# A two-layer decoder trunk on one core: the FFN's hidden tile turned by DMA in 16 bit halves in place of TensorE, tiles on multiples of 512 bytes, and a new rule for the pinned order

## The chip, the cores and the metric

The kernel runs on one core of a Trainium2 chip. A core has a matrix engine (TensorE, PE in the profile, with its weight loads as PEld), a vector engine (DVE), an activation engine (ACT), a general engine (POOL, nearly unused here) and a queue engine (SP) that issues most transfers. The metric is the device time of one execution in microseconds; smaller is better. A program of one core shows times that agree closely from run to run.

## The reference

The input x is 256 tokens by 2048 features, float32. There are two layers. Each adds a token mixer and then a dense SwiGLU FFN to the residual, with an RMS norm ahead of each; a last norm ends the trunk. Layer 0 mixes by causal pooling over windows of 2, 4, 8 and 16 tokens, layer 1 by differential attention with ALiBi.

```python
for i in range(DEPTH):
    hn = rmsnorm(h, norm_mix[i])
    mix = pool_mixer(...) if i % 2 == 0 else diff_attention(...)
    h = h + mix
    h = h + swiglu(rmsnorm(h, norm_ffn[i]), w_gate[i], w_up[i], w_down[i])
return rmsnorm(h, final_norm)

def swiglu(h, wg, wu, wd):          # wg, wu: 2048 x 5632, wd: 5632 x 2048
    return (jax.nn.silu(h @ wg) * (h @ wu)) @ wd
```

The FFNs hold most of the work: 176 of the 328 weight steps belong to gate and up, 88 to down.

## The kernel before

**Products.** Each weight matrix is read once, in steps of 1 MiB (`raw`, 128 partitions x 4 blocks x 512 columns): two slices of 128 rows of the weights, each with a left and a right 512 columns. Every operand is split into a high part, rounded for the fast float32 mode of TensorE, and a low part (what is left), and a product of two blocks is three matmuls: high by high, high by low, low by high (line 380). ACT rounds the high part (line 313), DVE subtracts it (line 314). A plain step is eight block products, 24 matmuls of 128x512. A step "by seven" follows Strassen's scheme: seven block products, 21 matmuls, for sums of weights that DVE makes (lines 319 to 321) and ACT and DVE split (lines 327, 328), and for sums of the activations made ahead. Which steps go by seven is fixed by lists, `GATE_UP`, `SEVEN_DOWN` and others, so that PE's time and DVE's are near each other.

**Groups.** `group` runs over the six or eight steps of one pair of 512 output columns and leaves eight PSUM banks; `combined` (lines 400 to 411: two copies on ACT, eight operations on DVE) makes four 128x512 blocks of them, `c11` to `c22`, for two halves of the tokens. The next group writes the same banks.

**FFN.** `ffn` goes over 11 groups of gate and up in chunks of 4, 4 and 3. After each group it computes silu(gate) on ACT (line 677) and the product with up on DVE (line 678), in token order, in place. The down product needs h with features on the partitions, so `pair` turns it: eight transposes of 128x128 on TensorE against the identity into a PSUM bank (line 450), then either ACT's cast and DVE's subtraction into the tile `h` (lines 454, 455), or, for a tile that will go by seven, two copies into `e` (line 463), three DVE operations for the sums (464 to 466), and the split (467, 468). A group makes two h tiles. After each chunk two groups of the down product run over the chunk's h tiles and are added to the residual `x_tok` (line 700). The same `pair` turns the residual ahead of the FFNs and attention, and attention's output.

**Buffers and queues.** Three `raw` buffers, three pairs of split weights, one set of sums. All weight loads are issued by SP (line 307). A load waits until DVE has read the buffer that it fills.

**Order.** The program's order is not that of the text. `in_order_of_need` reads the finished list of instructions, `steps_of` finds what depends on what, `walk` plays the list forward with fixed costs for each instruction, picking on each engine the ready instruction of lowest rank, and `due` works out by when each is needed, from PE's sequence. ACT, DVE and POOL are ranked by that due time, PE and SP by the order of the text. Two rounds are made, the shortest walk is kept, and its sequence is pinned on PE, DVE, ACT and SP. Each engine then runs its sequence strictly in turn, whatever becomes ready first on the chip.

**Places in memory.** Pools lie one behind the other. Those of the start (`st`) and of attention (`ap_`) begin with, or hold, small tiles: `counts` of 32 bytes a partition, `small` of 256.

Of the kernel before, what the change touches and what calls it, by code (L numbers as in the profile page):

```python
# [10 lines left out]
F32 = mybir.dt.float32  # L11
F32R = mybir.dt.float32r
AF = mybir.ActivationFunctionType
ALU = mybir.AluOpType
# [14 lines left out]
LATER = 70  # L29
ROUNDS = 2  # L30

# [22 lines left out]

A22, A21, A11, A12, S1, S3, S2, S4 = range(8)
T1, T3, T2, T4 = range(4)


# [5 lines left out]
LANDING = 2100  # L64
PER_MIB = 2500


class Step:

    def __init__(self, k, ins=None):  # L70
        self.k, self.ins, self.engine = k, ins, ins.engine if ins else POOL
        self.dma = bool(ins) and ins.opcode == "DMACopy"
# [6 lines left out]
        if self.dma:  # L79
            bytes_ = 4 * math.prod(c for _, c in ins.outs[0].ap)  # L80
            self.share = PER_MIB * bytes_ / 2 ** 20
            self.holds, self.lasts = (60 if self.engine == ACT else 330), LANDING + self.share
        elif self.engine == PE:
            n = size(ins.outs[0])
            one = 110 if ins.is_transpose else 14 + n / 2.4 if "float32r" in str(ins.ins[0].dtype) else 14 + n / 0.6
            self.holds, self.lasts = one, one + 163
        elif self.engine == DVE:
            if ins.opcode == "TensorScalarPtr":
                self.lasts = 185 + n / 0.96 if n > 8 else 159
            else:  # L90
                self.lasts = 152 + n / (1.92 if ins.opcode == "TensorCopy" else 0.96)
            self.holds = max(self.lasts - 80, 60)
        elif self.engine == ACT:
            self.lasts = 165 + n * 0.852
            if ins.opcode == "Activation" and any(hasattr(a, "ap") for a in list(ins.ins)[1:]):
                self.lasts += 100
            self.holds = max(self.lasts - 30, 60)
            if len(ins.outs) > 1:
                self.lasts, self.holds = self.lasts + 190, self.lasts + 160
        else:  # L100
            self.holds = self.lasts = 400


def steps_of(instructions):
# [3 lines left out]
    for ins in instructions:  # L108
# [15 lines left out]
        for writes, args in ((False, ins.ins), (True, ins.outs)):  # L124
            for a in args:
# [3 lines left out]
                t, dims = ap.tensor, [tuple(d) for d in ap.ap]  # L129
                first = ap.offset % dims[0][0]  # L130
                last = first + sum((c - 1) * s for s, c in dims[1:])
                alone = writes
                if t.space == PSUM:
                    first, last, alone = 0, 511, True
                if t.name not in seen:
# [76 lines left out]

def due(steps, start):

    by_start = sorted(steps, key=lambda s: start[s.k])
    at, clock = {}, 0.0
    for s in by_start:
        if s.engine == PE:
            at[s.k], clock = clock, clock + s.holds
    limit = [0.0] * len(steps)  # L220
    for s in reversed(by_start):
        limit[s.k] = min([limit[k] - s.lasts - SIGNAL[steps[k].engine] for k in s.after] + [at.get(s.k, clock)])
    return limit


def in_order_of_need(tc):

    steps = steps_of(list(tc.nc.cur_bb.bb.instructions))
    rank = [float(s.k) for s in steps]
    start, end = walk(steps, rank)  # L230
    for _ in range(ROUNDS):
# [14 lines left out]
def trunk_kernel(ctx, tc, x_n, gains, scale_in, final_in, subln, lam_in, band, counts_in, dist,  # L246
# [33 lines left out]
    ones = const.tile([P, P], F32, name="ones")  # L280
    nc.vector.memset(ones, 1.0)
    make_identity(nc, ident)
# [144 lines left out]

    def square_sum(ss, t, j):
# [16 lines left out]
    def pair(dst, src, gains, seven):  # L445

        ps = aux((P, 2, 2, P))
        for i in range(2):
            for t in range(2):
                nc.tensor.transpose(ps[:, i, 1 - t if seven else t], src(i, t), ident)  # L450
        if not seven:
# [9 lines left out]

        for i, at in ((0, slice(A21, A11 + 1)), (1, slice(A22, A12 + 1, A12 - A22))):
            nc.scalar.activation(e[:, at], ps[:, i], AF.Copy, scale=1.0 if gains is None else gains[i])
        nc.vector.tensor_tensor(e[:, S1:S3 + 1], e[:, A21:A11 + 1], e[:, A22:A21 + 1], ALU.subtract)
        nc.vector.tensor_tensor(e[:, S2], e[:, S1], e[:, A11], ALU.subtract)
        nc.vector.tensor_tensor(e[:, S4], e[:, A12], e[:, S2], ALU.add)
        nc.scalar.copy(dst[:, 0], e)  # L467
        nc.vector.tensor_tensor(dst[:, 1], e, f32(dst[:, 0]), ALU.subtract)

    def transposed(xp, j, gain, seven=()):  # L470
# [8 lines left out]
    with tc.tile_pool(name="start", bufs=1, reuse_waits="tile") as st:  # L479

        warm = tmp.tile([P, 8], F32, name="warm", bufs=1)
        nc.scalar.activation(warm[:, 0:1], ones[:, 0:1], AF.Sqrt)
# [35 lines left out]
        def squares(j):  # L518
            for t in range(2):
                square_sum(ss_in, t, j)  # L520

# [56 lines left out]
        def residual(g):  # L578

            cols = slice(g * 512, (g + 1) * 512)  # L580
            for t in range(2):
                z = st.tile([P, 512], F32, name="z", bufs=2)
                nc.vector.scalar_tensor_tensor(z, zp[g][t], counts[:, g, t:t + 1], scale_sb[:, cols], ALU.mult, ALU.mult)
                nc.vector.tensor_tensor(x_at(t, g * 512), z, x_at(t, g * 512), ALU.add)
                square_sum(ss, t, g)

# [41 lines left out]
    turn["of"] = 4  # L628
    nc.sync.dma_start(out=dist_sb, in_=dist)

    def finish(cs, ys, final_sb, ss):

        for t in range(2):
            part = tmp.tile([P, 64], F32, name="part", bufs=2)
            nc.vector.tensor_reduce(part[:, 0:1], ss[:, t, 0:2], AX.X, ALU.add)
            for b in range(2):
                for h in range(2):
                    first = 1024 + b * 512 + h * S
                    mine = slice(h * S, (h + 1) * S)
                    nc.vector.tensor_tensor(x_at(t, first, S), cs[t][b][:, mine], x_at(t, first, S), ALU.add)  # L640
                    sq = tmp.tile([P, 512], F32, name="sq", bufs=1)
# [15 lines left out]
    def ffn(layer, xq, ss, next_op, next_gain):  # L657
# [3 lines left out]
        with tc.tile_pool(name=f"ffn{layer}", bufs=1, reuse_waits="tile") as hp:  # L661
            g0 = 0
            ys = []
            for c, n in enumerate(CHUNKS):
# [6 lines left out]
                for g in range(g0, g0 + n):  # L671
# [3 lines left out]
                    for t in range(2):  # L675
                        gate, up = cs[t]
                        nc.scalar.activation(gate, gate, AF.Silu, scale=r[:, t:t + 1])  # L677
                        nc.vector.scalar_tensor_tensor(up, up, r[:, t:t + 1], gate, ALU.mult, ALU.mult)
                    for i in range(2):
                        at = 2 * (g - g0) + i  # L680
                        ht = hp.tile(pair_shape(at in SEVEN_DOWN), F32R, name="h", tag=f"h{at}")
                        pair(ht, lambda k, t: cs[t][1][:, (2 * i + k) * P:(2 * i + k + 1) * P], None, at in SEVEN_DOWN)
                        hp_tiles.append(ht)
                for o in range(2):
# [13 lines left out]
                    for b, t in ((0, 0), (0, 1), (1, 0), (1, 1)):  # L698
                        j = 2 * o + b
                        nc.vector.tensor_tensor(x_at(t, j * 512), cs[t][b], x_at(t, j * 512), ALU.add)  # L700
                        if last:
                            square_sum(ss_next, t, j)
                        if last and next_op is None:
# [15 lines left out]
    with tc.tile_pool(name="attn", bufs=1, reuse_waits="tile") as ap_, ExitStack() as heads:  # L719
        hq = heads.enter_context(tc.tile_pool(name="qk_sums", bufs=1, reuse_waits="tile"))  # L720
        at = heads.enter_context(tc.tile_pool(name="attn_tmp", bufs=2, reuse_waits="tile"))
        small = ap_.tile([P, 64], F32, name="small")
        qs_col, subln_sb, lam_sb, lp, le, neg_lam, gs = (
# [83 lines left out]
        for g in range(2):  # L807
            order, by_seven = LATE if g else EARLY
            cs = scaled(combined(group([(xp[p], p in by_seven, w_v[g, p]) for p in order], op_, bufs=1), op_), (r_col, r_col))
            for h in range(4 * g, 4 * g + 4):  # L810
# [6 lines left out]
                for t in range(2):  # L817
                    sq = tmp.tile([P, 512], F32, name="sq", bufs=1)[:, :E]
                    nc.scalar.activation(sq, op[:, t, :], AF.Square, accum_out=oss[:, t:t + 1])
# [7 lines left out]
        for g in range(2):  # L827
            cs = combined(group([(oT[p], p in SEVEN_O, w_o[g, p]) for p in range(NP)], op_, bufs=1), op_)
            for b in range(2):
                j = 2 * g + b  # L830
                for t in range(2):
                    nc.vector.tensor_tensor(x_at(t, j * 512), cs[t][b], x_at(t, j * 512), ALU.add)
                    square_sum(ss_next, t, j)
                transposed(xq, j, 4, SEVEN)
# [91 lines left out]
```

## Time and profile before

| | us |
|---|---|
| median of 3 runs | 1822.0 (1821.96 to 1822.05) |
| the profiled execution | 1821.8 |
| its span, first to last instruction | 1819.9 |
| start and pooling, to the first weight step of FFN 0 | about 39 |
| FFN 0 | about 39 to 738 |
| attention with its output product | about 738 to 1114 |
| FFN 1 and the end | about 1114 to 1820 |

In groups of instructions the columns are: line, engine, operation, tiles written and read, shape, count, then busy time and mean ns of one, then the engine's idle time ahead of them and what ended it. Matmuls overlap, so their mean is longer than the distance from one start to the next; the distance is read from the chain, where a run of matmuls stands as one piece with its length and count. In stretches, each engine has its busy time and, in brackets, the instructions that began in it. In waits the three numbers are the total in us, how many waits, and the longest. "SPq" is SP's queue of transfers; the row of an issue ends with KB of one transfer and the median us from issue to landing. TensorE's granted clock was 0.998 of full speed over the span.

### The profile page before, as it was taken

Reading aid. Unit: us, or ns where it says so; the run is one execution under the profiler, and the core shown is the slowest. Engines: PE = TensorE matmul, PEld = TensorE weight load, DVE = VectorE, ACT = ScalarE, POOL = GpSimd, SP = SyncE. Lnnn points to the kernel's source line nnn. Section 1 sums busy time; section 2 is a strip of 40 time slices with the busy share of each in tenths; the row PEclk is TensorE's granted clock in tenths of the full one; section 3 lists DMA queues with packets and bytes.
Section 4 is the critical chain, followed back from the end, with each engine's and each line's share of the span. In section 5 each row is a group of like instructions: output and inputs, shape, how many; then the busy total and the mean of one; then the engine's idle time right before and its main releaser. Section 6 shows DMA issues by size and latency. Waiting matters only on the chain.

```text
span 1819.9 us, 21122 instructions
## 1 busy us (share of the span) xinstructions
PE 1806.3 (99%) x8153; PEld 1487.6 (82%) x8153; DVE 1686.3 (93%) x1875; ACT 1084.0 (60%) x1170; POOL 0.7 (0%) x6
## 2 busy tenths in 40 slices
PE   9999999999999999999999999999999999999997
PEld 7888888888888888888888888888888888888886
DVE  7999999999999999989997889999999999999996
ACT  7656654565645566666666766665655556445663
POOL 0000000000000000000000000000000000000000
PEclk9999999999999999999999999999999999999999
DMA  6555555455555455635544445555555455555562
GB/s 267 208 185 207 187 208 208 185 208 215 201 209 187 182 208 185 225 145 185 185 176 172 184 165 194 196 208 185 214 207 203 185 208 192 210 222 192 196 220 109
DMA packets 50932, 356.37 MB, mean 196 GB/s; under 512 B 6160, under 2 KB 6288, under 8 KB 8464
## 3 DMA queue, kind: packets, MB, share of 16 engines
q1 hardware_dynamic: 49968, 353.40, 52.7%
q10 hardware_dynamic: 864, 1.63, 0.2%
q8 instruction: 64, 1.05, 0.2%
q14 instruction: 36, 0.29, 0.1%
HBM read 352.90 MB, written 2.10 MB: 195 GB/s over the span
## 4 chain that ended last, share of the span: by engine, by line
PE 98%; DVE 1%; ACT 1%; issue 0%; DVEq 0%; ACTq 0%
PE b L380 92%; PE b L450 2%; PE b L559 1%; PE b L555 1%; PE b L767 1%; PE b L798 0%; DVE wlo L314 0%; PE b L813 0%; PE b L485 0%; PE b L814 0%; PE b L530 0%; PE b L815 0%; DVE c L402 0%; DVE c L403 0%; PE b L752 0%
## 5 line engine op out<-in xcount | busy, mean ns | idle before, releaser
L380 PE MATMUL b<-whi,xp 128*128 128x512 f32 x2654 | 850.3, 392 | 0.4 <-ACT xp L467 0.3
L313 ACT CAST whi<-raw 128x1536 fp32r<-128x1536 f32 (+1 forms) x328 | 573.0, 1747 | 349.3 <-PE b L380 270.4
L314 DVE TENSOR_TENSOR wlo<-raw,whi 128x1536 fp32r<-128x1536 f32 (+1 forms) x328 | 681.3, 2077 | 69.6 <-ACT whi L313 68.4
L380 PEld LDWEIGHTS b<-whi,xp 128*128 128x128 f32 x2654 | 496.4, 188 | 104.9 <-DVE c L408 2.7
L380 PE MATMUL b<-wlo,xp 128*128 128x512 f32 x1327 | 520.1, 392 | 0.1
L327 ACT CAST thi<-tsum 128x1024 fp32r<-128x1024 f32 x254 | 266.3, 1052 | 183.9 <-DVE tsum L321 96.1
L380 PE MATMUL b<-whi,h 128*128 128x512 f32 x1108 | 349.2, 390 | 0.0
L328 DVE TENSOR_TENSOR tlo<-tsum,thi 128x1024 fp32r<-128x1024 f32 x254 | 306.5, 1216 | 2.3 <-ACT thi L327 2.0
L380 PEld LDWEIGHTS b<-wlo,xp 128*128 128x128 f32 x1327 | 249.2, 188 | 50.9 <-DVE wlo L314 0.5
L380 PE MATMUL b<-thi,xp 128*128 128x512 f32 x744 | 248.4, 390 | 0.0
L380 PEld LDWEIGHTS b<-whi,h 128*128 128x128 f32 x1108 | 207.6, 188 | 42.6 <-DVE c L408 0.2
L380 PE MATMUL b<-wlo,h 128*128 128x512 f32 x554 | 216.0, 390 | 0.1
L380 PEld LDWEIGHTS b<-thi,xp 128*128 128x128 f32 x744 | 139.4, 188 | 28.8 <-ACT thi L327 0.2
L319 DVE TENSOR_TENSOR tsum<-raw 128x1024 f32<-128x1024 f32 x127 | 154.5, 1216 | 0.6
L380 PE MATMUL b<-tlo,xp 128*128 128x512 f32 x372 | 144.9, 389 | 0.0
L380 PEld LDWEIGHTS b<-wlo,h 128*128 128x128 f32 x554 | 104.0, 188 | 21.9 <-DVE wlo L314 0.5
L320 DVE TENSOR_TENSOR tsum<-tsum,raw 128x512 f32<-128x512 f32 x127 | 86.7, 683 | 0.6
L321 DVE TENSOR_TENSOR tsum<-tsum,raw 128x512 f32<-128x512 f32 x127 | 86.7, 682 | 0.5
L380 PEld LDWEIGHTS b<-tlo,xp 128*128 128x128 f32 x372 | 69.8, 188 | 15.1
L380 PE MATMUL b<-thi,h 128*128 128x512 f32 x240 | 78.7, 389 | 0.0
L677 ACT ACTIVATE c<-c,r_tok 128x512 f32<-128x512 f32 x44 | 31.9, 724 | 63.1 <-DVE c L403 36.1
L380 PE MATMUL b<-whi,oT 128*128 128x512 f32 x216 | 69.0, 395 | 0.0
(148 smaller groups left out, 1230.7 us busy)
## 6 DMA issues: line engine op xcount, KB each, us to landing
raw<-w_gu SPq DMA_DIRECT2D x176, 1024.0 KB, 4.8
raw<-w_down SPq DMA_DIRECT2D x88, 1024.0 KB, 4.8
raw<-w_qk SPq DMA_DIRECT2D x32, 1024.0 KB, 4.8
raw<-w_v SPq DMA_DIRECT2D x16, 1024.0 KB, 4.8
raw<-w_o SPq DMA_DIRECT2D x16, 1024.0 KB, 4.7
x_tok<-x_n SPq DMA_DIRECT2D x4, 512.0 KB, 7.2
w<-pool_w SPq DMA_DIRECT2D x4, 512.0 KB, 7.7
raw<-pool_w SPq DMA_DIRECT2D x2, 1024.0 KB, 11.2
```

Source lines behind the costliest of these rows:

```text
L313: nc.scalar.copy(hi[:, lo_block:], raw[:, lo_block:])
L314: nc.vector.tensor_tensor(lo[:, lo_block:], raw[:, lo_block:], f32(hi[:, lo_block:]), ALU.subtract)
L319: nc.vector.tensor_tensor(s, raw[:, B11:B22 + 1], raw[:, B12:B12 + 1].broadcast_to([P, 2, 512]), ALU.add)
L320: nc.vector.tensor_tensor(t[:, 0], s[:, 0], raw[:, B22], ALU.add)
L321: nc.vector.tensor_tensor(t[:, 1], t[:, 0], raw[:, B21], ALU.add)
L327: nc.scalar.copy(hi, t)
L328: nc.vector.tensor_tensor(lo, t, f32(hi), ALU.subtract)
L380: nc.tensor.matmul(ps[b], x, y[:, block], start=first, stop=(left[b] == 0))
L450: nc.tensor.transpose(ps[:, i, 1 - t if seven else t], src(i, t), ident)
L555: nc.tensor.matmul(yp[g][t], a[:, rows], w_pool[g][:, at], start=(at == 0), stop=(at == 3))
L559: nc.tensor.matmul(yp[g][t], u, v[:, at], start=(at == 0 and j == 0), stop=(at == 3 and j == 2))
L677: nc.scalar.activation(gate, gate, AF.Silu, scale=r[:, t:t + 1])
```

## The change

1. In both FFNs h is no longer turned on TensorE. After the product with up, ACT copies the 128x512 block of floats, read as 16 bit halves, into the place of gate, low halves first and then high halves (`flip`). One DMA transpose, issued by SP, turns these 128 x 1024 halves into `turned`; a group has two, one for each half of the tokens. `pair_of_words` puts the halves together again by two ACT copies into `e` and goes on as before from there: cast and subtraction, or sums and split. All h tiles go through `e` now. The transposes of the residual and of attention's output stay on TensorE.
2. The eight slots of a tile that goes by seven have a new order.
3. `dist_sb` and `ones` move out of the constants, the tile `sq` out of `tmp`; squares are written to a tile of the start's pool, or over the block `c` just added to the residual; in the last group that is PSUM. `counts` and `small` are padded to 512 bytes a partition.
4. The order: `latest` plays the list backward from the end, engine by engine, in place of `due`. Eight rounds; in each, two ranks are tried, one with PE and SP by the order of the text, one with every engine by need, and the shorter walk goes on. Overlaps are found in bytes, the DMA transpose gets a cost, and ACT's reads with more than three dimensions get 80 ns more.

```diff
-ROUNDS = 2
+ROUNDS = 8
...
-A22, A21, A11, A12, S1, S3, S2, S4 = range(8)
+A12, A11, A21, A22, S3, S1, S2, S4 = range(8)
...
+PLACES = (slice(A11, A21 + 1), slice(A12, A22 + 1, A22 - A12))
...
+        if turns:
+            self.share = TURN_TILE * n * P / 2048
+            self.holds, self.lasts = 1290, 1000 + self.share
...
-def due(steps, start):
+def latest(steps, start):
+    missing = [len(s.after) for s in steps]
+    ready, place = [0.0] * len(steps), [0.0] * len(steps)
...
+        s = steps[-heapq.heappop(able[e])[1]]
+        place[s.k] = free[e] = now + s.holds
+        for k in s.before:
+            b = steps[k]
...
+            ready[k] = max(ready[k], place[s.k] + after)
...
+    end = max(place)
+    return [end - p for p in place]
...
     for _ in range(ROUNDS):
-        limit = due(steps, start)
-        rank = [float(s.k) if s.engine in (PE, SP) else limit[s.k] for s in steps]
-        again, span = walk(steps, rank)
+        need = latest(steps, last)
+        both = [[float(s.k) if s.engine in (PE, SP) else need[s.k] for s in steps], need]
+        last, span = min((walk(steps, r) for r in both), key=lambda w: w[1])
         if span < end:
-            start, end = again, span
+            start, end = last, span
...
-    dist_sb = const.tile([P, 2 * P], F32, name="dist_sb")
...
-        sq = tmp.tile([P, 512], F32, name="sq", bufs=1)
...
+    def half_words(ap):
+        return ap.bitcast(U16)
+
+    def flip(turned, t, gate, up):
+
+        halves_ = half_words(gate)
+        nc.scalar.copy(halves_.rearrange("p (w n) -> p w n", w=2), half_words(up).rearrange("p (n w) -> p w n", w=2))
+        nc.sync.dma_start_transpose(out=turned[:, t].rearrange("p w b n -> p (w b) n"), in_=halves_)
+
+    def pair_of_words(dst, turned, i, seven):
+
+        e = tmp.tile([P, 8, P], F32, name="e", bufs=1)
+        words = half_words(e).rearrange("p b (n w) -> p b n w", w=2)
+        if seven:
+            for k, at in enumerate(PLACES):
+                nc.scalar.copy(words[:, at], turned[:, :, :, 2 * i + k].rearrange("p t w n -> p t n w"))
+            seven_of(dst, e)
+            return
+        for k in range(2):
+            nc.scalar.copy(words[:, 2 * k:2 * k + 2], turned[:, :, :, 2 * i + k].rearrange("p t w n -> p t n w"))
+        both = e[:, :4].rearrange("p (k t) n -> p k (t n)", k=2)
+        nc.scalar.copy(dst[:, :, 0], both)
+        nc.vector.tensor_tensor(dst[:, :, 1], both, f32(dst[:, :, 0]), ALU.subtract)
...
-        counts = st.tile([P, 8], F32, name="counts")
+        counts = st.tile([P, 128], F32, name="counts")[:, :8]
...
-                    nc.scalar.activation(sq[:, :S], x_at(t, first, S), AF.Square, accum_out=part[:, at:at + 1])
+                    nc.scalar.activation(cs[t][b][:, mine], x_at(t, first, S), AF.Square, accum_out=part[:, at:at + 1])
...
                         nc.vector.scalar_tensor_tensor(up, up, r[:, t:t + 1], gate, ALU.mult, ALU.mult)
+                        if t == 0:
+                            turned = hp.tile([P, 2, 2, 4, P], U16, name="turned")
+                        flip(turned, t, gate, up)
...
-                        pair(ht, lambda k, t: cs[t][1][:, (2 * i + k) * P:(2 * i + k + 1) * P], None, at in SEVEN_DOWN)
+                        pair_of_words(ht, turned, i, at in SEVEN_DOWN)
...
-        small = ap_.tile([P, 64], F32, name="small")
+        small = ap_.tile([P, 128], F32, name="small")
+        dist_sb = ap_.tile([P, 2 * P], F32, name="dist_sb")
+        nc.sync.dma_start(out=dist_sb, in_=dist)
+        ones = all_ones(ap_)
```

More of the change, by code (lines that the diff above doesn't have):

```diff
@@ L12 @@
 F32R = mybir.dt.float32r
+U16 = mybir.dt.uint16
 AF = mybir.ActivationFunctionType
@@ L65 @@
 PER_MIB = 2500
+TURN_TILE = 14
 class Step:
@@ L71, in __init__ @@
         self.k, self.ins, self.engine = k, ins, ins.engine if ins else POOL
-        self.dma = bool(ins) and ins.opcode == "DMACopy"
+        turns = bool(ins) and ins.opcode == "DmaTransposeAnt"
+        self.dma = turns or bool(ins) and ins.opcode == "DMACopy"
         self.before, self.after, self.reads = set(), [], set()
@@ L78, in __init__ @@
         n = max(size(a) for a in list(ins.outs) + list(ins.ins) if hasattr(a, "ap"))
-        if self.dma:
+        if turns:
+            self.share = TURN_TILE * n * P / 2048
+            self.holds, self.lasts = 1290, 1000 + self.share
+        elif self.dma:
             bytes_ = 4 * math.prod(c for _, c in ins.outs[0].ap)
@@ L97, in __init__ @@
             self.holds = max(self.lasts - 30, 60)
+            if len(list(ins.ins[0].ap)) > 3:
+                self.lasts += 80
             if len(ins.outs) > 1:
@@ L129, in steps_of @@
                 t, dims = ap.tensor, [tuple(d) for d in ap.ap]
-                first = ap.offset % dims[0][0]
-                last = first + sum((c - 1) * s for s, c in dims[1:])
+                each = mybir.dt.size(a.dtype)
+                first = ap.offset % dims[0][0] * each
+                last = first + sum((c - 1) * s for s, c in dims[1:]) * each + each - 1
                 alone = writes
                 if t.space == PSUM:
-                    first, last, alone = 0, 511, True
+                    first, last, alone = 0, 2047, True
                 if t.name not in seen:
@@ L210, in walk @@
     return start, max(free.values())
-def due(steps, start):
[L215 to L223, printed above, removed]
+def latest(steps, start):
+    missing = [len(s.after) for s in steps]
+    ready, place = [0.0] * len(steps), [0.0] * len(steps)
+    engines = (PE, DVE, ACT, SP, POOL)
+    free = {e: 0.0 for e in engines}
+    able, coming = {e: [] for e in engines}, {e: [] for e in engines}
+    for s in steps:
+        if not s.after:
+            heapq.heappush(coming[s.engine], (0.0, s.k))
+    for _ in steps:
+        now, e = min((free[e] if able[e] else max(free[e], coming[e][0][0]), i)
+                     for i, e in enumerate(engines) if able[e] or coming[e])
+        e = engines[e]
+        while coming[e] and coming[e][0][0] <= now:
+            k = heapq.heappop(coming[e])[1]
+            heapq.heappush(able[e], (-start[k], -k))
+        s = steps[-heapq.heappop(able[e])[1]]
+        place[s.k] = free[e] = now + s.holds
+        for k in s.before:
+            b = steps[k]
+            if b.engine != e or b.dma:
+                after = b.lasts + SIGNAL[e] - (0 if b.dma else b.holds)
+            elif e == DVE or e == ACT and k in s.reads:
+                after = b.lasts + SETTLES[e] - b.holds
+            else:
+                after = 0.0
+            ready[k] = max(ready[k], place[s.k] + after)
+            missing[k] -= 1
+            if not missing[k]:
+                heapq.heappush(coming[b.engine], (ready[k], k))
+    end = max(place)
+    return [end - p for p in place]
 def in_order_of_need(tc):
@@ L230, in in_order_of_need @@
     start, end = walk(steps, rank)
+    last = start
     for _ in range(ROUNDS):
-        limit = due(steps, start)
-        rank = [float(s.k) if s.engine in (PE, SP) else limit[s.k] for s in steps]
-        again, span = walk(steps, rank)
+        need = latest(steps, last)
+        both = [[float(s.k) if s.engine in (PE, SP) else need[s.k] for s in steps], need]
+        last, span = min((walk(steps, r) for r in both), key=lambda w: w[1])
         if span < end:
-            start, end = again, span
+            start, end = last, span
     order = mybir.DependencyInfo(mybir.DependencyClass.NoSync, mybir.DependencyReason.DATA)
@@ L277, in trunk_kernel, with all_ones @@
     gain_sb = const.tile([P, 6, NK], F32, name="gain_sb")
-    dist_sb = const.tile([P, 2 * P], F32, name="dist_sb")
     ident = const.tile([P, P], F32, name="ident")
-    ones = const.tile([P, P], F32, name="ones")
-    nc.vector.memset(ones, 1.0)
+    def all_ones(pool):
+        ones = pool.tile([P, P], F32, name="ones")
+        nc.vector.memset(ones, 1.0)
+        return ones
     make_identity(nc, ident)
@@ L426, in rsqrt, with square_sum @@
         return r
-    def square_sum(ss, t, j):
-        sq = tmp.tile([P, 512], F32, name="sq", bufs=1)
+    def square_sum(ss, t, j, sq):
         nc.scalar.activation(sq, x_at(t, j * 512), AF.Square, accum_out=ss[:, t, j:j + 1])
@@ L449, in pair @@
             for t in range(2):
-                nc.tensor.transpose(ps[:, i, 1 - t if seven else t], src(i, t), ident)
+                nc.tensor.transpose(ps[:, i, t], src(i, t), ident)
         if not seven:
@@ L460, in pair, with seven_of @@
         e = tmp.tile([P, 8, P], F32, name="e", bufs=1)
-        for i, at in ((0, slice(A21, A11 + 1)), (1, slice(A22, A12 + 1, A12 - A22))):
+        for i, at in enumerate(PLACES):
             nc.scalar.activation(e[:, at], ps[:, i], AF.Copy, scale=1.0 if gains is None else gains[i])
-        nc.vector.tensor_tensor(e[:, S1:S3 + 1], e[:, A21:A11 + 1], e[:, A22:A21 + 1], ALU.subtract)
+        seven_of(dst, e)
+    def seven_of(dst, e):
+        nc.vector.tensor_tensor(e[:, S3:S1 + 1], e[:, A11:A21 + 1], e[:, A21:A22 + 1], ALU.subtract)
         nc.vector.tensor_tensor(e[:, S2], e[:, S1], e[:, A11], ALU.subtract)
@@ L479, in trunk_kernel @@
     with tc.tile_pool(name="start", bufs=1, reuse_waits="tile") as st:
+        ones = all_ones(st)
         warm = tmp.tile([P, 8], F32, name="warm", bufs=1)
@@ L519, in squares @@
             for t in range(2):
-                square_sum(ss_in, t, j)
+                square_sum(ss_in, t, j, st.tile([P, 512], F32, name="sq"))
         def turned(g):
@@ L584, in residual @@
                 nc.vector.tensor_tensor(x_at(t, g * 512), z, x_at(t, g * 512), ALU.add)
-                square_sum(ss, t, g)
+                square_sum(ss, t, g, st.tile([P, 512], F32, name="sq"))
         def onward(g):
@@ L628, in trunk_kernel @@
     turn["of"] = 4
-    nc.sync.dma_start(out=dist_sb, in_=dist)
     def finish(cs, ys, final_sb, ss):
@@ L701, in ffn @@
                         if last:
-                            square_sum(ss_next, t, j)
+                            square_sum(ss_next, t, j, cs[t][b])
                         if last and next_op is None:
@@ L817, in trunk_kernel @@
                 for t in range(2):
-                    sq = tmp.tile([P, 512], F32, name="sq", bufs=1)[:, :E]
+                    sq = at.tile([P, E], F32, name="sq", bufs=1)
                     nc.scalar.activation(sq, op[:, t, :], AF.Square, accum_out=oss[:, t:t + 1])
@@ L832, in trunk_kernel @@
                     nc.vector.tensor_tensor(x_at(t, j * 512), cs[t][b], x_at(t, j * 512), ALU.add)
-                    square_sum(ss_next, t, j)
+                    square_sum(ss_next, t, j, cs[t][b])
                 transposed(xq, j, 4, SEVEN)
```

2 lines of the change are left out of this document (1 added, 1 removed).

## The prediction

> **What bounds the kernel now.** I read first the busy times and the chain of work that ended last, then the groups of instructions with shapes kept apart, then the busy time by stretches whose ends are those of the matmul groups.
>
> ```profile
> span 1819.9 us, 21122 instructions
> PE 1806.3 (99%) x8153; PEld 1487.6 (82%) x8153; DVE 1686.3 (93%) x1875; ACT 1084.0 (60%) x1170; POOL 0.7 (0%) x6
> PE 98%; DVE 1%; ACT 1%; issue 0%; DVEq 0%; ACTq 0%
> PE b L380 92%; PE b L450 2%; PE b L559 1%; PE b L555 1%; PE b L767 1%; PE b L798 0%; DVE wlo L314 0%; PE b L813 0%; PE b L485 0%; PE b L814 0%; PE b L530 0%; PE b L815 0%; DVE c L402 0%; DVE c L403 0%; PE b L752 0%
> ...
> 92.20 40.01 PE b L380 x176
> 132.90 0.66 PE b L450 x6
> ```
>
> PE carries 98% of the chain, nearly all of it the products of line 380, and 2% the transposes of line 450. The last two rows are pieces of the chain in order of time: a product takes 40.01/176 = 0.227 us of PE, a transpose 0.66/6 = 0.110 us. A busy PE need not be PE at its peak, so I look for what PE would need if nothing else counted. The stretches give it: one row for each group of eight weight steps (a step without sums is 24 products, a step by seven products is 21).
>
> ```profile
> core 0: us, PE busy (x) PEld busy (x) DVE busy (x) ACT busy (x) POOL busy (x), PEclk, DMA share, GB/s
> 85.70:254.20 168.50, 168.50 (x760) 139.27 (x759) 163.30 (x164) 99.08 (x89) 0.00 (x0) 1.00 0.54 199
> 254.20:295.70 41.50, 41.50 (x185) 34.38 (x184) 37.87 (x37) 20.90 (x16) 0.00 (x0) 1.00 0.55 203
> 295.70:336.50 40.80, 40.80 (x182) 33.80 (x181) 39.57 (x36) 23.35 (x19) 0.00 (x0) 1.00 0.54 207
> 336.50:378.30 41.80, 41.80 (x189) 34.56 (x188) 40.35 (x40) 24.93 (x22) 0.00 (x0) 1.00 0.54 201
> 378.30:547.40 169.10, 169.02 (x757) 139.72 (x756) 157.62 (x153) 92.83 (x81) 0.00 (x0) 1.00 0.56 202
> 588.30:738.00 149.70, 149.70 (x681) 123.79 (x680) 145.55 (x152) 91.75 (x95) 0.00 (x0) 1.00 0.54 197
> 738.00:1114.50 376.50, 375.12 (x1744) 308.93 (x1743) 329.13 (x481) 246.19 (x356) 0.00 (x0) 1.00 0.49 181
> 1157.70:1327.00 169.30, 169.06 (x759) 139.22 (x758) 163.73 (x164) 99.17 (x89) 0.00 (x0) 1.00 0.54 199
> 1661.10:1777.70 116.60, 116.60 (x527) 96.22 (x526) 112.89 (x114) 68.28 (x64) 0.00 (x0) 1.00 0.55 199
> ```
>
> The rows from 295.7 and from 336.5 are two gate-and-up groups with four steps by seven, 4 x 21 + 4 x 24 = 180 products or 40.85 us each. The first has no transposes of h in it and takes 40.8 us: PE has no gap at all. The second has eight and takes 41.8. So eight transposes cost 1.0 us there, with what they disturb. The row from 254.2 (3 x 21 + 5 x 24 = 183 products, 41.52 us) takes 41.5: no gap again. In the FFNs PE is the bound, but DVE is close behind: 163.30 of 168.50 us in the first row. How close, its waits in that stretch tell:
>
> ```profile
> DVE wlo L314 <- ACT whi L313: 2.2, 2, 1.2
> DVE c L402 <- PE b L380: 1.9, 2, 1.0
> ```
>
> DVE waits 4.1 of the 168.5 us, so it needs 164.4 by itself.
>
> **The change part by part.**
>
> Removed: the TensorE transposes of h, in both FFNs.
>
> ```profile
> L450 PE MATMUL b<-ident,c 128*128 128x128 f32 x176 | 26.3, 272 | 0.0
> L454 ACT CAST h<-b 128x512 fp32r<-128x512 f32 x28 | 16.0, 593 | 9.5 <-PE b L450 9.5
> L463 ACT ACTIVATE e<-b 128x256 f32<-128x256 f32 x32 | 10.6, 382 | 17.7 <-PE b L450 17.7
> L327 ACT CAST thi<-tsum 128x1024 fp32r<-128x1024 f32 x254 | 266.3, 1052 | 183.9 <-DVE tsum L321 96.1
> L405 ACT COPY c<-b 128x512 f32<-128x512 f32 x41 | 24.0, 586 | 5.0 <-PE b L380 4.8
> ```
>
> By the chain's pitch 176 x 0.110 = 19.4 us; by the two twin groups 176/8 = 22 times 1.0 = 22.0 us. I take 0.95 a group, 20.9 us, all of it on the path, since PE ends its queue last.
>
> Late next is DVE. In the first row PE would need 168.5 - 4 x 0.95 = 164.7, DVE 164.4. The like stretches from 588.3, 1157.7 and 1661.1 are as full (DVE busy 97% in each). The four hold 14 of the 22 groups. In the other eight (four of them in the row from 378.3, DVE 157.62 of 169.10, 93%) DVE has room. With two engines equal and three buffers between them each will sometimes wait for the other. The loss lies between 0 and the 14 x 0.95 = 13.3 us; I take a quarter, **+3.3 us**, as the twin group from 295.7 ran without a gap with DVE at 39.57 of 40.80.
>
> DVE's own work stays: the same sums and subtractions, of the same sizes, read from e in place of PSUM.
>
> Added on ACT: 44 copies of 1024 halves each (nearest row 128x1024, 1.052 us): 46 us. The 28 plain h tiles get two copies of 512 halves (0.586 each) ahead of the cast: 33 us. The 16 others have two copies of 512 where 256 words were scaled: 2 x (0.586 - 0.382) x 16 = 7 us. Together 86 us, 3.9 a group, against the 41.8 - 24.9 = 16.9 us that ACT is idle in the group from 336.5. The trace has no 16 bit copy with such strides: at best nothing lost, at worst each microsecond falls ahead of a cast that DVE waits for, 86 us. Nearest is the wait of 2.2 us in four groups above, so ACT is mostly early. I take **+1 us**; were the cover gone (three times the duration, ACT full), it would be tens.
>
> Added on SP: 44 DMA transposes of 128 x 1024 halves, 256 KB each, two a group, in the queue of the weight loads. h of the last group of a chunk is needed only after six steps of the down product, over 30 us later, so their own latency is hidden. What counts is whom they hold up: a transpose waits on SP for ACT's copy, and behind it wait the loads.
>
> ```profile
> SPq L307 <- DVE wlo L314: 916.1, 198, 13.3
> raw<-w_gu SPq DMA_DIRECT2D x176, 1024.0 KB, 4.8
> ACT whi L313 <- DMA raw<-w_gu: 17.5, 20, 1.9
> q1 hardware_dynamic: 49968, 353.40, 52.7%
> q10 hardware_dynamic: 864, 1.63, 0.2%
> ...
> 602.93 1.22 DVE L319 TENSOR_TENSOR tsum<-raw 128x1024 f32<-128x1024 f32 x1
> 607.48 0.68 DVE L321 TENSOR_TENSOR tsum<-tsum,raw 128x512 f32<-128x512 f32 x1
> ```
>
> SP mostly waits for a free buffer (198 times, 4.6 us on average). There are three raw buffers and a step takes 41.8/8 = 5.2 us, so a buffer comes round in 15.7 us; a load takes 4.8, the use of it 5.2 (602.93 to 608.16). That leaves some 5 us by which a load may be late before the path feels it, though 20 casts waited for one already, 17.5 us in all. What a transpose holds the queue is not in the trace. From below: 256 KB at the pace of q1 (353.40 MB in 52.7% of 16 engines' 1819.9 us) is 0.7 us. From above: its output is 1024 pieces of 256 bytes; at q1's 0.307 us a packet, 64 a DMA engine, 19.6 us. Nearest are the small packets of q10: 0.2% of 16 x 1819.9 over 864 is 0.067 us, times 64 gives 4.3 us, for pieces seven times as large. I take 1 to 4 us, under the 5 of slack: **0**.
>
> Two rules of the Trainium skill pull apart here. "VectorE: DVE Perf Modes", The three transpose paths, has 390 ns for a 128x128 on TensorE and 1309 ns through DMA, and its rules for kernel authors prefer TensorE where PSUM will do; this trace has 0.110 us on TensorE, not 0.39. Eight blocks in a row would by that page be an estimated 10.5 us a transpose. "DMA: Bandwidth & Descriptors", Latency and other measured facts, has 261 GB/s for a DMA transpose, an estimated 1.0 us. No run shown has either.
>
> Order and addresses. New addresses touch the tiles of the start and of attention.
>
> ```profile
> L380 PE MATMUL b<-whi,xp 128*128 128x512 f32 x2654 | 850.3, 392 | 0.4 <-ACT xp L467 0.3
> L559 PE MATMUL b<-whi,xt_hl 128*128 128x512 f32 x40 | 13.7, 412 | 0.0
> ```
>
> The start's products take 412 ns where those of line 380 take 392: if the address is the reason, 60 of them win 20 ns each, 1.2 us; if not, nothing. The order is computed anew for all engines, PE included. Where only order and addresses change there is little to win: PE is idle 1.4 us from 738 to 1114.5. What a worse order costs is a rival below. The last squares go to c or to PSUM in place of sq, by the same instruction. From -3 to the rival's +41 I take **-1**, near the rows.
>
> Sum: 1819.9 - 20.9 + 3.3 + 1 - 1 = 1802.3 us of span. The profiled execution took 1821.8, 1.9 outside the span, and the median of the runs is 1822.0, 0.2 more: 1802.3 + 2.1 = **1804 us**, -1.0%. Own range 1797 to 1811.
>
> **The rivals.**
>
> *DVE takes the bound.* For: its floor is within 0.3 us of PE's new one in the first row. Against: eight groups have room. All 13.3 us lost: 1804 + 10 = 1814. If ACT's 3.9 us a group also fall ahead of DVE by a fifth (0.8 x 22 = 17), all of the gain is gone, 1822, and the change has only moved the wait.
>
> *The transposes hold up the loads* (slower). Place: SP's queue, twice a group. Price: what a transpose holds the queue beyond 5 us is lost, as DVE has no spare time to catch up; 44 x (X - 5). It decides from X = 5.4, where 18 us are eaten. At X = 6 it is 1804 + 44 = 1848, at 19.6 far beyond 2000. For: the estimate by small packets, 4.3, is close to 5, and casts wait for loads even now. Against: the DMA share is 0.54, and q10's packets are larger. By the page's 10.5 us it would be 1804 + 242.
>
> *The new order is worse* (slower). A combination of a group is a chain of DVE work that PE's banks wait for; one put 1 us too late at each of the 41 boundaries is +41, 1845. Against: the present order, made in the same way, leaves PE without a gap.
>
> *The new order is better*: attention and start give 4 us and DVE keeps up, 1804 - 7 = 1797 or below.
>
> **How the numbers follow.** Forecast 0.58; better than 1797: 0.08; DVE takes part, 1811 to 1818: 0.10; takes all: 0.07; loads held up 0.13; order worse 0.04. A measurement here tells 0.2% from no change (1818.4 to 1825.6). Faster 0.58 + 0.08 + 0.10 = 0.76, same 0.07, slower 0.17. The range, 1794 to 1830, leaves out some 0.04 below and 0.14 above.
>
> **What would show it.** Right: no PE rows of line 450 reading c; the groups that took 41.8 and 42.4 us now near 41 and 41.6; DVE at 97% or more in those stretches; ACT near 1170 us; transposes landing within 5 us of issue. DVE the bound: stretches as long as before, with PE waiting for wlo or tlo. Loads held up: ACT's waits for raw grown from 17.5 us to far more, DMA landing times over 5. Wrong altogether: PE gaps at the group boundaries, or time lost in attention, where nothing but order and addresses changed.

## The result and the profile after

The changed kernel takes 1800.69 us (1800.27 to 1800.86), before 1821.98 (1821.96 to 1822.05): a ratio of 0.9883, interval 0.9866 to 0.9900, 21.3 us faster. The profiled execution has a span of 1799.1 us.

Lines of the page of the changed kernel, with busy times by engine, queue q1 (packets, MB, share of the sixteen DMA engines), and the chain by engine:

```profile
span 1799.1 us, 20991 instructions
PE 1785.8 (99%) x7977; PEld 1471.3 (82%) x7977; DVE 1679.4 (93%) x1876; ACT 1167.5 (65%) x1270; POOL 0.7 (0%) x6
...
q1 hardware_dynamic: 96432, 364.94, 58.2%
...
PE 72%; DVE 3%; ACT 1%; issue 1%; DMA 1%; DVEq 0%; SPq 0%; ACTq 0%
```

PE's busy time fell by 20.5 us and ACT's rose by 83.5. DVE's fell by 6.9 though it runs the same operations: the lengths of all its instructions add up to 1812.0 us before and 1810.8 now, but 1648 of them in place of 1577 start before the one ahead has ended, and such overlaps are counted once. Queue q1 moves 11.5 MB more, in 46,464 more packets. The chain could be followed back only to 370 us, about 79% of the span, so PE's 72% are to be compared with that and not with the 98% of before; over the last groups of either FFN it runs through DVE and ACT.

The busy time of the changed kernel in stretches, whose ends are again those of the groups; the columns are those of the rows in the prediction:

```profile
core 0: us, PE busy (x) PEld busy (x) DVE busy (x) ACT busy (x) POOL busy (x), PEclk, DMA share, GB/s
85.00:249.60 164.60, 164.60 (x728) 136.28 (x728) 161.68 (x164) 115.22 (x109) 0.00 (x0) 1.00 0.64 217
249.60:291.00 41.40, 41.40 (x184) 34.31 (x183) 38.82 (x38) 21.12 (x16) 0.00 (x0) 1.00 0.56 209
291.00:331.80 40.80, 40.80 (x181) 33.79 (x181) 39.16 (x39) 23.15 (x19) 0.00 (x0) 1.00 0.55 197
331.80:372.80 41.00, 41.00 (x181) 33.58 (x181) 40.81 (x41) 29.26 (x28) 0.00 (x0) 1.00 0.62 211
372.80:539.20 166.40, 166.19 (x733) 137.34 (x732) 156.54 (x152) 104.21 (x93) 0.00 (x0) 1.00 0.62 215
580.00:727.80 147.80, 147.59 (x661) 121.70 (x659) 144.42 (x153) 103.41 (x111) 0.00 (x0) 1.00 0.62 210
727.80:1104.00 376.20, 374.85 (x1741) 309.00 (x1740) 327.65 (x481) 245.90 (x352) 0.00 (x0) 1.00 0.50 180
1147.30:1312.20 164.90, 164.90 (x727) 136.05 (x726) 162.72 (x167) 116.16 (x109) 0.00 (x0) 1.00 0.64 217
```

The first four groups took 168.5 us and take 164.6; the twin group with transposes took 41.8 and takes 41.0, beside 40.8 for the one without, which has not changed. Attention took 376.5 and takes 376.2. So nearly all of the gain lies in the two FFNs: FFN 0 ended at 738.0 and ends at 727.8 (10.2 us), the rest of the program, from 1114.5 to 1819.9 before and from 1104.0 to 1799.1 now, gives 10.3. DVE is now at 98% in the first row, 99.5% in the row from 331.8, and PE is busy all of the time in these rows of the FFNs, but for 0.2 us in those from 372.8 and 580.

The new instructions, from the groups by form and the issues of the changed kernel; the first two rows are the copies of halves, the third the issue of the DMA transpose, whose last number is the us to landing:

```profile
L514 ACT COPY c<-c 128x1024 uint16<-128x1024 uint16 x44 | 45.5, 1043 | 10.1 <-DVE c L739 10.0
L527 ACT COPY e<-turned 128x512 uint16<-128x512 uint16 x56 | 35.8, 679 | 6.5 <-DVE h L506 3.9 <-DMA turned<-c 1.3 <-DVE h L530 1.2
turned<-c SPq DMA_TRANSPOSE x44, 2.8
```

And how long SP itself is busy with one, from the view of the tile `turned` (min/median/max in ns, first and last start):

```profile
L515 SPq DMA_TRANSPOSE turned<-c x44: 1232/1238/1979, 111.5 to 1732.9; - x44
```

A transpose holds SP for 1.24 us and lands 2.8 us after its issue (median; the latest 6.6). By q1's share it costs the DMA engines (0.582 x 1799.1 - 0.527 x 1819.9) / 44 = 2.0 us of all sixteen. Not all of that is its own. In the trace's list of packets the transposes have 45,056 packets of 256 bytes with a mean of 20.9 ns, 1.3 us of sixteen engines for each transpose; the rest is that the packets of the plain loads take 365 ns in the mean in place of 355. So it is a third of the prediction's estimate of 4.3 us from q10's packets, and far under its upper bound of 19.6.

### The profile page after: what moved, and what is told of

Read it like the earlier page. It is cut to its first block, busy times and chain, and to the rows that moved or that the text cites. A ratio compares the mean times of both kernels' runs of the same rounds, so it can differ in the third digit from the quotient of the medians.

```text
span 1799.1 us, 20991 instructions
## 1 busy us (share of the span) xinstructions
PE 1785.8 (99%) x7977; PEld 1471.3 (82%) x7977; DVE 1679.4 (93%) x1876; ACT 1167.5 (65%) x1270; POOL 0.7 (0%) x6
## 4 chain that ended last, share of the span: by engine, by line
PE 72%; DVE 3%; ACT 1%; issue 1%; DMA 1%; DVEq 0%; SPq 0%; ACTq 0%
PE b L416 70%; DVE wlo L350 1%; PE b L834 1%; PE b L485 1%; ACT whi L349 1%; PE b L865 0%; DVE tlo L364 0%; DMA turned<-c 0%; DMA raw<-w_gu 0%; DVE tsum L355 0%; DMA raw<-w_qk 0%; PE b L880 0%; PE b L881 0%; DVE tsum L357 0%; ACT c L514 0%
## 5 line engine op out<-in xcount | busy, mean ns | idle before, releaser
L416 PE MATMUL b<-thi,xp 128*128 128x512 f32 x744 | 254.2, 390 | 0.0
L416 PEld LDWEIGHTS b<-thi,h 128*128 128x128 f32 x240 | 45.0, 188 | 9.4
```

The costliest lines, as they stand in the source:

```text
L416: nc.tensor.matmul(ps[b], x, y[:, block], start=first, stop=(left[b] == 0))
```

## The experiments

All are the changed kernel with one thing altered (one of them the run with the old rule of order). The order is worked out from the finished list of instructions, so where an alteration adds or removes instructions, the order of all of them is another one too. Beside each stands its median, its range, and its ratio to the kernel before with the interval.

**h on TensorE again, all else new.**

```diff
-                        if t == 0:
-                            turned = hp.tile([P, 2, 2, 4, P], U16, name="turned")
-                        flip(turned, t, gate, up)
...
-                        pair_of_words(ht, turned, i, at in SEVEN_DOWN)
+                        pair(ht, lambda k, t: cs[t][1][:, (2 * i + k) * P:(2 * i + k + 1) * P], None, at in SEVEN_DOWN)
```

> The changed kernel with h turned on TensorE again, by the same helper as before; order rule, addresses and slot order stay new. Theory (the gain is the PE time of the 176 transposes): about 20 us come back, 1820 to 1823 us, groups with transposes at 41.8 and 42.4 us again. Rival (the new order rule made the gain, and the DMA turn is free but worth little): 1801 to 1812 us.

1820.70 us (1820.53 to 1820.95), ratio 0.9993 (0.9983 to 1.0002). Order, slots and addresses by themselves cannot be told from no change; 20.0 of the 21.3 us come back with the transposes. As the theory had it. The transposes of h in this run, and the twin group that takes 41.0 us in the changed kernel and 41.8 again here:

```profile
L485 PE MATMUL b<-ident,c 128*128 128x128 f32 x176 | 26.4, 272 | 0.0
336.30:378.10 41.80, 41.60 (x188) 34.08 (x187) 40.44 (x40) 24.80 (x22) 0.00 (x0) 1.00 0.56 201
```

**The DMA turn with the old rule of order.**

```diff
-ROUNDS = 8
+ROUNDS = 2
...
-        need = latest(steps, last)
-        both = [[float(s.k) if s.engine in (PE, SP) else need[s.k] for s in steps], need]
-        last, span = min((walk(steps, r) for r in both), key=lambda w: w[1])
+        limit = due(steps, start)
+        rank = [float(s.k) if s.engine in (PE, SP) else limit[s.k] for s in steps]
+        again, span = walk(steps, rank)
```

> The changed kernel with the old order rule (due times, two rounds, PE and SP by the order of the text). Theory: the FFN groups stay at PE's own time, so 1799 to 1804 us. Rival (with DVE as full as it is now, only the backward walk keeps PE without a gap): the third of a microsecond of DVE's margin is lost in each of the 14 full groups and more, 1805 to 1815 us.

1817.58 us (1815.96 to 1819.48), ratio 0.9977 (0.9967 to 0.9987). Neither number: the old rule loses 16.9 us, more than the rival had. The DMA turn alone is worth 4.4 us, the order alone 1.3 (with slots and addresses, and too little to be told from nothing), the two together 21.3. Where it is lost shows in a stretch of one group, three of its eight steps by seven (41.52 us for PE alone), in the run with the old rule:

```profile
626.40:670.40 44.00, 42.15 (x185) 34.26 (x185) 42.97 (x43) 28.87 (x27) 0.00 (x0) 1.00 0.63 222
```

The chain of the same run in the stretch from 628 to 680, in order of time (start, us, what):

```profile
626.82 2.20 DVE wlo L327
629.02 0.60 DVE c L419
629.62 1.15 DVE tsum L332
...
630.84 1.05 ACT thi L340
631.90 0.04 issue
631.94 43.86 PE b L393 x193
```

PE's next products wait for a high part of a sum (`thi`), ACT waits for the sum, and DVE made the sum only after a low part and a step of the combination. DVE is busy 42.97 of the 44.00 us, more than the 41.52 that PE needs: the old rule puts more of DVE's work into this stretch than fits beside PE, and work ahead of the sum that PE is waiting for. Over the whole run DVE has about the same to do under either rule (busy 1683.6 and 1679.4 us). That stretch is followed in detail. PE's longest waits for DVE and ACT in its products point the same way, first in the run with the old rule, then in the changed kernel; but they do not add up to all of the 16.9 us.

```profile
PE b L393 <- DVE wlo L327: 5.8, 5, 2.1
PE b L393 <- DVE c L421: 2.1, 3, 0.7
PE b L393 <- ACT thi L340: 2.0, 2, 1.0
```

```profile
PE b L416 <- DVE c L439: 1.1, 1, 1.1
PE b L416 <- DVE wlo L350: 0.2, 1, 0.2
```

**Which part of the new rule.** Three runs: PE and SP ranked by the order of the text only; the old due times with eight rounds; the new rule with two rounds.

```diff
-        both = [[float(s.k) if s.engine in (PE, SP) else need[s.k] for s in steps], need]
+        both = [[float(s.k) if s.engine in (PE, SP) else need[s.k] for s in steps]]
```

> The changed kernel with the backward walk and eight rounds, but PE and SP ranked by the order of the text in every round. Theory A (the backward walk's limits for DVE and ACT are what keeps DVE's work in time): 1800 to 1804 us. Theory B (PE and SP must be free to follow the need): 1810 to 1818 us, near the 1817.6 of the old rule.

1807.60 us (1805.89 to 1807.87), ratio 0.9919 (0.9904 to 0.9934): between the two theories. Of the 16.9 us between the rules the backward limits for DVE and ACT give 10.0, letting PE and SP follow the need 6.9. Each run shows the one order that its rule found, so these are the shares of these orders; how far they hold for the rules in general was not tried.

```diff
-ROUNDS = 2
+ROUNDS = 8
...
-        limit = due(steps, start)
+        limit = due(steps, last)
...
-        again, span = walk(steps, rank)
+        last, span = walk(steps, rank)
```

(against the run with the old rule; each round starts from the walk before)

> The changed kernel with the old due times, but eight rounds, each from the walk before. Theory A and B alike (the rule of need matters, not how often it is tried): 1812 to 1819 us. Rival (two rounds were too few): 1800 to 1805 us.

1817.62 us (1816.58 to 1819.83), ratio 0.9978 (0.9969 to 0.9988): the number of rounds does nothing for the old rule.

```diff
-ROUNDS = 8
+ROUNDS = 2
```

> The changed kernel with two rounds in place of eight. Theory (the rule of need matters, not the number of rounds): 1800 to 1805 us. Rival (the rounds found the order): over 1808 us.

1807.03 us (1806.73 to 1807.33), ratio 0.9917 (0.9901 to 0.9934). The expectation missed by 2 us: with the new rule the six rounds more are worth 6.3 us.

**Old addresses.**

```diff
-        counts = st.tile([P, 128], F32, name="counts")[:, :8]
+        counts = st.tile([P, 8], F32, name="counts")
...
-        small = ap_.tile([P, 128], F32, name="small")
+        small = ap_.tile([P, 64], F32, name="small")
```

> The changed kernel with counts at 32 bytes and small at 256 bytes a partition again, so that the tiles behind them lie off the multiples of 512. Theory: the start's products of line 622 go back from 402 to about 412 ns, 60 of them by some 7 ns from start to start, 0.4 us in all: 1800.5 to 1801.5 us. Rival (addresses matter for attention too): over 2 us more, 1803 us and up.

1800.84 us (1800.23 to 1801.61), ratio 0.9884 (0.9870 to 0.9899): 0.15 us, inside the spread. The groups of the start's products, first with the old places, then in the changed kernel:

```profile
L622 PE MATMUL b<-whi,xt_hl 128*128 128x512 f32 x40 | 13.4, 408 | 0.0
L622 PE MATMUL b<-wlo,xt_hl 128*128 128x512 f32 x20 | 7.9, 396 | 0.0
```

```profile
L622 PE MATMUL b<-whi,xt_hl 128*128 128x512 f32 x40 | 13.2, 402 | 0.0
L622 PE MATMUL b<-wlo,xt_hl 128*128 128x512 f32 x20 | 7.8, 390 | 0.0
```

Each matmul is 6 ns shorter with its tiles on multiples of 512 bytes. There are 60 of them; more than that does not show. The other moves of tiles were not undone.

**DVE and ACT given more.** The low part of every h tile subtracted twice (44 more operations on DVE), and the copy of halves made three times over (88 more on ACT).

```diff
-        nc.vector.tensor_tensor(dst[:, :, 1], both, f32(dst[:, :, 0]), ALU.subtract)
+        for _ in range(2):
+            nc.vector.tensor_tensor(dst[:, :, 1], both, f32(dst[:, :, 0]), ALU.subtract)
...
             seven_of(dst, e)
+            nc.vector.tensor_tensor(dst[:, 1], e, f32(dst[:, 0]), ALU.subtract)
```

> The changed kernel with the low part of every h tile subtracted twice on DVE, with the same result: 28 x 0.60 + 16 x 1.14 = 35 us of DVE work at its start-to-start pace, none of it ahead of anything urgent. Theory (in chunks of full groups DVE has only some 1 to 3 us left to itself, in the others 6 or more): 4 to 12 us slower, 1805 to 1813 us, all of it in the first and last chunks. Rival A (DVE is the bound already): nearly all 35 us, 1825 us and up. Rival B (DVE has room everywhere): 1800 to 1802 us.

1809.21 us (1808.63 to 1809.41), ratio 0.9929 (0.9914 to 0.9944): 8.5 of some 35 us are lost (DVE's busy time rose by 32.0), the rest found room. DVE is close to the bound and is not the bound. Whether the loss lies in the first and last chunks, as expected, was not followed.

```diff
+        for _ in range(3):
-        nc.scalar.copy(halves_.rearrange("p (w n) -> p w n", w=2), half_words(up).rearrange("p (n w) -> p w n", w=2))
+            nc.scalar.copy(halves_.rearrange("p (w n) -> p w n", w=2), half_words(up).rearrange("p (n w) -> p w n", w=2))
```

> The changed kernel with the copy of halves made three times over, 88 more copies of 1.04 us on ACT, 92 us in all, 4.2 a group. Theory (ACT's work is under its idle time, 12 us a group): within 3 us, 1800 to 1804 us. Rival (an ACT copy in the wrong place delays a cast that DVE waits for, and DVE has no room): a fifth or more of it is lost, 1819 us and up.

1802.81 us (1802.35 to 1802.96), ratio 0.9894 (0.9879 to 0.9909): 92 us more on ACT cost 2.1, 0.12%, which is hardly to be told from nothing.

**More transposes in SP's queue.** Two and three times the same transpose to the same place, each waiting for the landing of the one before; and a spare one behind each, to the block of the product with up, which nobody reads any more.

```diff
+        for _ in range(2):
-        nc.sync.dma_start_transpose(out=turned[:, t].rearrange("p w b n -> p (w b) n"), in_=halves_)
+            nc.sync.dma_start_transpose(out=turned[:, t].rearrange("p w b n -> p (w b) n"), in_=halves_)
```

> The changed kernel with each DMA transpose issued three times over, to the same place, so that SP holds 3 x 1.24 = 3.7 us for each block and the last lands some 8 us after the first is issued. Theory (a load may be late by some 5 us before the path feels it): within 1.5 us of the changed kernel, 1800 to 1802 us. Rival (loads are the edge already, each late microsecond is lost): 2 x 2 x 22 x 1.24 / 2 = 55 us or more, 1850 us and up; half of that if only a part of the loads is late.

> The changed kernel with each DMA transpose issued twice to the same place; the second waits on SP until the first has landed, so SP is held for 2.8 + 1.24 = 4.1 us, where three held it for 2 x 2.8 + 1.24 = 6.9 us and cost 106 us. Theory (late loads cost what is beyond a slack, 106 / 44 = 2.4 us of 6.9, so the slack is 4.5 us): within 5 us of the changed kernel, 1800 to 1806 us. Rival (no slack, each microsecond that SP is held beyond one transpose costs the same 106 / 5.6 = 19 us): 1800.7 + 2.8 x 19 = 1854 us.

Three: 1907.12 us (1905.24 to 1907.51), ratio 1.0466 (1.0450 to 1.0481), 106 us lost. Two: 1841.56 us (1840.42 to 1842.71), ratio 1.0107 (1.0092 to 1.0122), 41 us lost. Both expectations of the theory fell; three came out beyond the rival's 55 us, two 12 us short of the rival's 1854. But these two make h late as well, and ACT stands in its pinned place waiting for it; so a third run.

```diff
         nc.sync.dma_start_transpose(out=turned[:, t].rearrange("p w b n -> p (w b) n"), in_=halves_)
+        nc.sync.dma_start_transpose(out=half_words(up).rearrange("p (b n) -> p b n", n=P), in_=halves_)
```

> The changed kernel with a second, spare DMA transpose behind each real one, of the same halves into the block of the product with up, which nobody reads any more. SP is held twice 1.24 us with no wait for a landing between, and the real transpose lands as before, so that ACT's copies of its halves are not late. It tells the two causes of the slow runs with two and three transposes in a row apart. Theory (ACT stood in its pinned place waiting for halves that land late, 50 us against 12, and loads have some slack): within 6 us of the changed kernel, 1800 to 1807 us. Rival (each microsecond that SP is held beyond one transpose is lost by the loads, as 41 us for 2.8): 1800.7 + 1.24 x 14.6 = 1819 us or more.

1819.87 us (1817.80 to 1823.75), ratio 0.9989 (0.9980 to 0.9999): 19.2 us lost, as the rival had it. The profiled execution, 1823.75 us, is the slowest of the ten. ACT's waits for transfers, first in the changed kernel, then with the spare transpose (us in total, times, longest):

```profile
ACT whi L349 <- DMA raw<-w_gu: 14.8, 13, 3.2
ACT e L523 <- DMA turned<-c: 11.2, 5, 3.9
ACT whi L349 <- DMA raw<-w_down: 3.3, 2, 2.2
ACT e L527 <- DMA turned<-c: 1.3, 1, 1.3
```

```profile
ACT whi L349 <- DMA raw<-w_gu: 40.0, 23, 5.4
ACT e L524 <- DMA turned<-c: 23.7, 11, 6.4
ACT whi L349 <- DMA raw<-w_down: 10.7, 5, 2.6
ACT e L528 <- DMA turned<-c: 4.2, 3, 3.7
```

And pieces of the chain of the run with the spare transpose:

```profile
366.09 6.80 DMA raw<-w_gu
...
597.90 8.43 DMA raw<-w_gu
...
1720.46 8.84 DMA raw<-w_gu
```

ACT's waits for weights grow from 18.1 to 50.7 us, and loads that land after 6.7 to 8.8 us stand in the chain, while the median of all loads stays at 4.9. A second transpose in a row is therefore felt by the loads. Waits for `turned` grow too, from 12.5 to 27.9, so how the 19.2 us part between the two was not settled. Two more things are open. A spare transpose takes time of the DMA engines as well as of SP, and the run does not part them. And the order of this run is not that of the changed kernel: DVE's sequence differs, and an order alone was worth up to 16.9 us above, so some of the 19.2 may be the order's. With two and three chained transposes the waits for weights are 41.4 and 132.1 us, those for `turned` 50.0 and 45.9: by these waits the late h weighs more with two, the loads with three.

**One more step by seven.** In FFN 0 DVE idles 9.9 us in the four groups of the row from 372.8 (156.54 busy of 166.40); a step by seven in gate-and-up group 7, which is one of them, uses that, and the same is done in FFN 1.

```diff
-(2, 4, 5, 6), (2, 4, 6), (2, 4, 6), (2, 4, 5, 6), (2, 4, 5, 6), (2, 4, 6)]
+(2, 4, 5, 6), (2, 4, 6), (2, 4, 5, 6), (2, 4, 5, 6), (2, 4, 5, 6), (2, 4, 6)]
```

(the end of both lists of `GATE_UP`)

> The changed kernel with one more step by seven in gate-and-up group 7 of either FFN, which takes three products of 0.227 us from PE (0.68 us a layer) and adds some 4.3 us to DVE in a chunk where it idles 10 us or more. Theory: 1.4 us faster, 1799.0 to 1800.0 us. Rival (DVE's room is not there when it is needed): the same or slower, 1800.7 to 1804 us.

1799.41 us (1799.02 to 1799.53), ratio 0.9875 (0.9859 to 0.9892): 1.3 us less than the changed kernel, about the 1.4 that six products of 0.227 us make. The two ranges do not meet, but their intervals do: a difference this small is not told for certain. It is the lowest median of the kernels run here.

## Why the prediction came out

It said 1804 us; 1800.7 was measured, within its own range of 1797 to 1811.

- **The transposes removed, -20.9 us.** Borne out: the stretch for which 168.5 - 3.8 = 164.7 us was worked out takes 164.6. The 20.0 us that come back with the transposes are this term less what the DMA turn costs on DVE, ACT and the queue together.
- **DVE next, +3.3 us.** This is the term that was mis-sized. If the removal is worth its 20.9, the 20.0 leave 0.9 us for DVE, ACT and the queue, where the sum had 4.3; that is nearly all of the miss of 3.7. PE takes 41.0 us in the group where DVE is at 99.5%, 0.2 more than in its twin. What was off is the premise that the two engines are equal. DVE was said to need 164.4 us by itself in the first row, the stretch less DVE's waits. In the changed kernel its waits in the same four groups are these:

```profile
DVE tlo L364 <- ACT thi L363: 1.2, 1, 1.2
DVE c L438 <- PE b L416: 0.9, 1, 0.9
DVE wlo L350 <- ACT whi L349: 0.5, 1, 0.5
```

That is 2.6 of 164.6 us, so by the same reckoning the same number of instructions (164) now needs 162.0: with fewer pauses more of them overlap. DVE had 1.6% to spare, not nothing. The doubled subtraction shows the same: little to spare, but some.
- **Order, -1 us as a term of its own.** Wrong as a term, and that its size by itself is near (1.3 us, not told from none) is luck. The sum treated DVE's loss and the order as independent. They aren't: with the old rule and the DMA turn 16.9 us are lost, more than the 13.3 that the DVE term had as its upper end, and the time is 1817.6, outside the prediction's range. With the order of the new rule DVE's loss is nearly nothing. So the forecast held by a part of the change that it valued at 1 us. The prediction looked for gains of the order where PE was idle; the gain is that PE does not become idle.
- **ACT, +86 us of work for +1.** Measured 83.5 us of work. The copies take 1043 ns (1052 taken) and 679 (586 taken). The cover holds: 92 us more cost 2.1.
- **The DMA transposes, 0, with some 5 us of slack for the loads.** The price was in the range taken, 1.24 us of SP and 1.3 to 2.0 of the DMA engines (1 to 4 taken), and with one transpose a block it is hidden, or nearly. The slack looks far too large. It came from the mean time in which a buffer comes round, and the mean says nothing of the loads that had no lead before (20 casts waited for one already). With one more transpose in the same place 19.2 us were lost, by late loads, late halves and another order together. The rival of the loads held up was nearer than its 0.13 says: it was put to decide from 5.4 us of holding, and two transposes in a row, 2 x 1.24, came with the loss of nearly all of the gain.
- **The Trainium skill's two figures.** By "VectorE: DVE Perf Modes", The three transpose paths, eight blocks in a row would have been 10.5 us; the whole transfer lands in 2.8. By "DMA: Bandwidth & Descriptors", Latency and other measured facts, 261 GB/s would make 1.0 us of 256 KB; the packets of the transposes take 1.3 us of sixteen engines, some 196 GB/s. The measured value lies between, near the second.
- **Addresses, 0 to 1.2 us.** 0.15, inside the spread; 6 ns on each of 60 matmuls. The 1.2 counted 20 ns for all 60, but only 40 of them took 412 ns; the other 20 took 396.

## What to carry to other kernels

When the bound engine is relieved and the next is within two per cent of it, ask first what sets the order on that next engine: the same relief was worth 4.4 us under one rule of order and 20.0 under another. The mean time round its buffers did not tell a queue's slack here; put one more transfer into the queue and see, and hold the order fixed when you do, which was not done here. Nor was an engine's need its stretch less its waits: with fewer pauses the same work took less. Work moved to an engine that idled 40% of a group (16.9 of 41.8 us) was as good as free here, and what it took is read from the nearest row of the same number of elements.

## What the hardware showed that was not expected

- Two engines both ran at 98% or more of a stretch of 165 us without PE losing anything, with three buffers between them: PE's 164.6 us are its products alone, while DVE is busy 161.68.
- A DMA transpose of 128 x 1024 halves in SBUF makes 1056 packets (46,464 more in q1 over 44) and takes 1.3 us of all sixteen DMA engines (58.9 us over 44, by the packets of 256 bytes), some 196 GB/s. It lands 2.8 us after its issue, where a plain load of four times the bytes lands in 4.8 to 4.9 us.
- ACT's copy of 512 halves took 679 ns where 512 floats take 586; of 1024 halves 1043, where 1024 floats take 1051. The first reads two halves that lie far apart for each word, the second walks in long rows; that this is the reason was not tried.
